# A two-layer decoder trunk on one core: the first layer's output projection of seven token tiles in partial sums in SBUF, beside the last attention pair

## The chip, the cores and the metric

The kernel runs on one core of one Trainium2 chip. The metric is the device time of one execution in microseconds (us). The engines are named as in the profile: PE (TensorE matmuls; PEld its weight loads), DVE (VectorE), ACT (ScalarE), POOL (GpSimd) and SP (SyncE, which here issues every DMA). Each engine works through its own queue in order; semaphores order the queues among each other.

## The reference

1024 tokens of width 1024 pass two layers and a final norm. Layer 0 is causal attention with a forget gate (16 heads of 64), layer 1 a sparse attention ("NSA") with three branches. What matters here is the seam between them:

```
h = rmsnorm(x, norm_g[0]); proj = h @ w_in          # q, k, v, forget gate f, z
o = softmax(q k^T / 8 + c_q - c_k, causal) @ v       # c: running sum of log sigmoid(f)
x = x + (o * silu(z)) @ w_out                        # output projection of layer 0
h = rmsnorm(x, norm_g[1]); proj = h @ nsa_w_in       # layer 1 begins; its first sections are kc and vc
```

## The kernel before, in words

Every float32 product is made of float32r matmuls: an operand is split into a high part (a cast on ACT) and a low part (a subtraction on DVE or POOL), and `mm3` issues three matmuls, hi·hi, hi·lo and lo·hi, into one PSUM bank. Tokens lie in eight tiles t = 0 to 7 of 128; tiles 4 to 7 are half 1, tiles 0 to 3 half 0. A bank holds 128 x 512 float32.

Layer 0's attention goes over eight head pairs p, two heads j each, four query duos x each; a duo joins a long and a short query tile. For each duo PE makes the scores S (six matmuls), DVE adds the gate bias and finds the row minimum (`P`, `m`), ACT takes the exponential and the high part, DVE the low part `hl`, a DMA transposes `hl` into `pT`, and two duos later PE multiplies by v (`O`, 18 matmuls); DVE then scales into `o`. After a pair's last duo PE transposes `o` (`pto`), DVE multiplies with silu(z), and a DMA writes the rows to `oF` in DRAM ("z" in the profile).

Two generators are merged: `fox_main` (the attention) and `fox_fill` (projections k, v, q, z of later pairs, then the weights `wo` of the output projection, then a part of that projection, `out_start`). `merge` takes steps of the filler until their summed cost reaches a ratio (`PACE` = 2.3, and `LAST` = 2.6 for the last eight duos) times the cost of the main steps. A step of the filler may be a condition that blocks it until it holds. Tile's scheduler then sets the final order within each queue.

The output projection needs for a token tile all eight 128-row chunks of `oF`, one per pair: 2 halves of the columns x 8 chunks x 3 = 48 matmuls (named `y`). `out_start` makes for tiles 4 and 5 chunks 0 to 3, then 4 to 6, for tile 6 chunks 0 to 6, and after the last pair chunk 7 of the three. Their sums stay in PSUM all that time, four of its eight banks while scores are still made and six at the end: tile 4 in a bank of `psA` and one of `psS`, tile 5 in `psA` and `psT`, tile 6 in two of `psS`. The attention shares the same pools (S in `psS`, O in `psA`, transposes in `psT`). The other five tiles follow in `out_layer`, behind the attention: load of 8 chunks of `oF` (`of`), split (`ohi`, `olo`), 48 matmuls, addition of x (`xr`, on DVE out of PSUM), sum of squares on ACT, root, reciprocal, two multiplications `h_n` on DVE, then eight transposes (`pth_n`) and their split into `hT` (ACT high, DVE low), which is the input of layer 1. `out_layer` serves layer 1's projection as well. Layer 1 starts with sections `kc` 0, `kc` 1 (PSUM `pn_kc`), each over half 1 and then half 0, 24 matmuls a time; then the gates (`pg`).

Of the kernel before, what the change touches and what calls it, by code (L numbers as in the profile page):

```python
# [19 lines left out]
D = 1024  # L20
S = 1024
# [19 lines left out]
def tile_fox_nsa(ctx, tc, a, out):  # L41
# [216 lines left out]
    hp = tc.alloc_tile_pool(name="hT0", bufs=1, side="right")  # L258
    st = tc.alloc_tile_pool(name="start", bufs=1, side="right")
# [66 lines left out]
    def fox_k(p):  # L326
        KH = [sa.tile([P, S], F32R, tag="KH", bufs=4, name=f"KH_{p}_{j}") for j in range(2)]
        KL = [sa.tile([P, S], F32R, tag="KL", bufs=4, name=f"KL_{p}_{j}") for j in range(2)]
# [111 lines left out]
    def fox_fill():  # L440
        for p in range(8):
# [24 lines left out]
    def out_start():  # L466


        ys = ready["ys"] = {}
        ws = {}  # L470

        def split(t, c, src):
            oh, ol = ws[t]
            A.copy(oh[:, c, :], src)
            V.tensor_tensor(ol[:, c, :], src, f(oh[:, c, :]), OP.subtract)

        def rows_of(t, c):
            yield lambda: ("o", c.stop - 1, 1) in ready
            of = wp.tile([P, KC, P], F32, tag="wst", bufs=1, name=f"of0{t}_{c.start}")
            dma(of[:, c, :], oF[c.start * P:c.stop * P, t * P:(t + 1) * P].rearrange("(k p) t -> p k t", p=P))  # L480
            split(t, c, of[:, c, :])

        def products(t, c):
            oh, ol = ws[t]
            for half in range(2):
                for k in range(c.start, c.stop):
                    wh, wl = ready["wout"][k // 4]
                    cs = slice(half * 512, half * 512 + 512)
                    mm3(ys[t][half], oh[:, k, :], ol[:, k, :], wh[:, k % 4, cs], wl[:, k % 4, cs], k == 0, k == KC - 1)
                    yield 650  # L490

        for t, banks in ((4, (ps_a, ps_s)), (5, (ps_a, ps_t))):
            ws[t] = out_parts(f"0{t}")
            ys[t] = [ps(f"y0_{t}_{half}") for half, ps in enumerate(banks)]
            yield from rows_of(t, slice(0, 4))
# [987 lines left out]
```

## Time and profile before

| | |
|---|---|
| median of 3 runs | 1527.96 us (1526.06 to 1528.8) |
| the profiled execution | 1529.59 us, of which the span of the profile is 1527.8 us |
| busy in the span | PE 1421.9, DVE 1066.2, ACT 805.1, POOL 565.1 us |
| granted TensorE clock over the span | 0.974 |
| 40 to 480 us (attention of layer 0 with its projections) | PE busy 439.17 of 440 us |
| 480 to 590 us (its end) | PE busy 90.12 of 110 us |
| 590 to 672 us (output projection, norms, start of layer 1) | PE busy 74.67 of 82 us |

A group's row gives the busy time, the mean time of one instruction in ns and the idle time of the engine just before it, with what ended that. PE's busy time counts each matmul from its start to its modelled end, and successive matmuls overlap; the distance from start to start is what a matmul costs in a row of them. "PEclk" is the clock that TensorE was granted, as a share of full speed.

### The profile page before, as it was taken

The page shows a single profiled execution, that of the slowest core. Times are in us where ns is not written, and L with a number is a line of the kernel's source. Part 1 is how long each engine was busy: PE and PEld are TensorE (multiplying, and loading weights), DVE is VectorE, ACT ScalarE, POOL GpSimd, SP SyncE. Part 2 cuts the span into 40 slices and gives each one's busy share as a digit, 9 for nine tenths or more (in the row PEclk, how much of TensorE's full clock was granted, in tenths as well). Part 3 has the DMA queues.
Part 4 walks back from the last instruction along what each step waited for, and adds up shares of the span by engine and source line. Part 5 has one row for each costly group of instructions (what it writes and reads, how often), then busy time and mean ns, then how long its engine had stood idle before and what let it go on. Part 6 is the DMA issues. An engine that isn't in the chain of part 4 may idle for free.

```text
span 1527.8 us, 29541 instructions
## 1 busy us (share of the span) xinstructions
PE 1421.9 (93%) x10488; PEld 1179.8 (77%) x10488; DVE 1066.2 (70%) x2759; ACT 805.1 (53%) x2028; POOL 565.1 (37%) x604
## 2 busy tenths in 40 slices
PE   5999999999999778999999899999999999988698
PEld 4888888888788556878888777778888888876576
DVE  6586878788787864457554668677888788888143
ACT  5364646646565652224131664476767676676031
POOL 1232222222322600033333332366767766575000
PEclk9999999999999979999999998999999999999799
DMA  7796777866777765342435577586777857766442
GB/s 254 238 180 142 163 158 157 182 153 143 172 165 166 178 124 197 121 136 83 156 98 163 148 187 201 180 184 133 180 152 146 204 124 144 189 142 147 132 151 83
DMA packets 405812, 242.72 MB, mean 159 GB/s; under 512 B 332513, under 2 KB 353889, under 8 KB 405409
## 3 DMA queue, kind: packets, MB, share of 16 engines
q1 hardware_dynamic: 405664, 240.84, 64.8%
q8 instruction: 83, 1.36, 0.4%
q14 instruction: 65, 0.52, 0.1%
HBM read 120.96 MB, written 44.11 MB: 108 GB/s over the span
## 4 chain that ended last, share of the span: by engine, by line
PE 63%; DVE 16%; ACT 8%; DMA 6%; issue 4%; POOL 1%; SPq 1%; POOLq 0%; DVEq 0%; ACTq 0%
PE S_n L1275 5%; PE y L133 3%; PE y L135 3%; PE y L134 3%; PE ptp_n L1307 3%; ACT P_n L1285 2%; DVE P_n L1282 2%; PE v L133 2%; PE v L135 2%; PE v L134 2%; DVE hl L605 2%; PE S L585 2%; ACT P L603 2%; PE k L133 2%; PE k L134 2%
## 5 line engine op out<-in xcount | busy, mean ns | idle before, releaser
L1285 ACT ACTIVATE P_n<-P_n,m_n 128x640 f32<-128x640 f32 (+7 forms) x256 | 187.2, 732 | 68.5 <-DVE m_n L1282 34.4
L1275 PE MATMUL S_n<-nk,nq 128*128 128x320 f32 (+5 forms) x768 | 180.0, 350 | 8.6 <-DVE m_n L1282 8.3
L603 ACT ACTIVATE P<-P,m 128x512 f32<-128x512 f32 (+1 forms) x192 | 116.9, 610 | 131.4 <-DVE m L594 130.7
L574 POOL TENSOR_TENSOR Bd<-B,tri 128x128 f32<-128x128 f32 x128 | 62.3, 502 | 245.8 <-DVE m L594 227.5
L1289 POOL TENSOR_TENSOR hl_n<-P_n,hl_n 128x640 f16<-128x640 f32 (+4 forms) x128 | 145.0, 1133 | 9.8
L1275 PEld LDWEIGHTS S_n<-nk,nq 128*128 128x128 f32 x768 | 125.2, 193 | 20.9 <-DVE m_n L1282 10.8
L605 DVE SCALAR_TENSOR_TENSOR hl<-P,hl 128x512 f16<-128x512 f32 (+1 forms) x192 | 124.6, 667 | 20.5 <-ACT hl L604 19.5
L1282 DVE CUSTOM_DVE_ANT_0 P_n<-S_n,wmask 128x640 f32<-128x640 f32 (+2 forms) x192 | 113.4, 595 | 25.7 <-PE S_n L1275 16.0
L1288 POOL CAST hl_n<-P_n 128x640 f16<-128x640 f32 (+4 forms) x128 | 77.0, 601 | 122.1 <-ACT P_n L1285 107.8
L150 ACT ACTIVATE pth_n<-ptp_n 128x512 f16<-128x512 f32 (+1 forms) x160 | 85.9, 547 | 49.9 <-PE ptp_n L1307 48.8
L133 PE MATMUL y<-wo,ohi 128*128 128x512 f32 x240 | 97.5, 406 | 15.4 <-ACT ohi L697 13.9
L151 DVE SCALAR_TENSOR_TENSOR ptl_n<-ptp_n,pth_n 128x512 f16<-128x512 f32 (+1 forms) x160 | 99.9, 632 | 15.4 <-ACT pth_n L150 13.9
L1307 PE MATMUL ptp_n<-ident,P_n 128*128 128x128 f32 x576 | 92.4, 281 | 9.4 <-DVE ptl_n L151 4.3
L135 PE MATMUL y<-wo,olo 128*128 128x512 f32 x240 | 95.9, 402 | 0.8 <-DVE olo L698 0.8
L134 PE MATMUL y<-wo,ohi 128*128 128x512 f32 x240 | 96.0, 400 | 0.0
L604 ACT ACTIVATE hl<-P 128x512 f16<-128x512 f32 (+1 forms) x192 | 92.5, 513 | 4.5 <-DMA pT<-hl 3.1
L1307 PEld LDWEIGHTS ptp_n<-ident,P_n 128*128 128x128 f32 x576 | 66.9, 143 | 20.8 <-DVE ptl_n L151 9.5
L585 PE MATMUL S<-KH,Q 128*128 128x512 f32 (+1 forms) x192 | 68.1, 368 | 11.3 <-DVE m L594 10.9
L1315 PE MATMUL O_n<-nv,pth_n 128*128 128x64 f16 x576 | 72.0, 196 | 6.5 <-ACT pth_n L150 5.5
L727 DVE TENSOR_TENSOR xr<-y,xr 128x512 f32<-128x512 f32 x32 | 21.5, 689 | 73.5 <-PE y L135 65.6
L1315 PEld LDWEIGHTS <-pth_n 128*128 128x128 f16 x576 | 52.2, 98 | 25.3 <-ACT pth_n L150 11.1
L1316 PE MATMUL O_n<-nv,pth_n 128*128 128x64 f16 x576 | 71.0, 194 | 0.0
(384 smaller groups left out, 4566.0 us busy)
## 6 DMA issues: line engine op xcount, KB each, us to landing
nq<-qD SPq DMA_DIRECT2D x64, 256.0 KB
B<-cD SPq DMA_DIRECT2D x16, 512.0 KB
wo<-wD SPq DMA_DIRECT2D x16, 512.0 KB
nq<-qD SPq DMA_DIRECT2D x64, 128.0 KB
of<-oF SPq DMA_DIRECT2D x11, 512.0 KB
x<-in_x_dram SPq DMA_DIRECT2D x8, 512.0 KB
wst_k<-in_fox_w_dram SPq DMA_DIRECT2D x8, 512.0 KB
wst_v<-in_fox_w_dram SPq DMA_DIRECT2D x8, 512.0 KB
```

Of the source, the lines that this page charges most:

```text
L133: T.matmul(ps, wh, mh, start=first, stop=False, **kw)
L134: T.matmul(ps, wh, ml, start=False, stop=False, **kw)
L135: T.matmul(ps, wl, mh, start=False, stop=last, **kw)
L151: V.scalar_tensor_tensor(lo[:, 0:n], pt[:, 0:n], scale, h, OP.mult, OP.subtract)
L603: A.activation(L[:, 0:n], L[:, 0:n], AF.Exp, bias=init, scale=-1.0, accum_out=self.lr[:, col + c:col + c + 1])
L605: V.scalar_tensor_tensor(lo[:, cs], L[:, 0:n], UP, hi[:, cs], OP.mult, OP.subtract)
L1275: T.matmul(ps[:, b, 0:w], self.q[x][:, qi * P:(qi + 1) * P], k[:, k0 + b * w:k0 + b * w + w], start=(x == 0), stop=(x == 1))
L1282: V.tensor_tensor_reduce(dst, src, mk, 1.0, 3e38, OP.add, OP.min, m)
L1285: A.activation(L, L, AF.Exp, bias=m, scale=-1.0, accum_out=self.l[:, y, qi:qi + 1])
L1289: G.tensor_tensor(hl[:, n:2 * n], L, hl[:, 0:n], OP.subtract)
L1307: T.transpose(pt[:, (x + i) * P:(x + i + 1) * P], L[:, kb * P - k0:(kb + 1) * P - k0], ident)
L1315: T.matmul(o, hi, v[:, 0:64], start=first, stop=False)
```

## The change

The partial sums no longer wait in PSUM. For each part of the projection (tiles 4 to 7 with chunks 0 to 3, tiles 4 to 7 with chunks 4 to 6, tiles 0, 1, 2 with chunks 0 to 6: eleven parts) the sum goes into a bank of `psA`, and DVE adds it at once to the tile's x row in SBUF (`xs0[t]`, loaded beforehand into the buffers of keys no longer needed, for which `KH` and `KL` move to a pool `sk` of their own that lives longer). Behind the attention stands `out_rest`: for tiles 4, 5, 6, 7 chunk 7 alone, for tile 3 all eight chunks, for tiles 0, 1, 2 chunk 7, with the norm of each tile. The rows of the last pair are loaded once, as two halves (`o7h`, `o7l`), rather than taken from `z` or read back with each tile. The weights `wo` are split with every second subtraction on DVE rather than all on POOL, and the load of their first half moves between two projections. `LAST` goes, and `merge` gets a cap. In layer 1 `kc` 0 and 1 (and `vc` 0 and 1) become one section each: half 1 of both, then half 0 of both.

```diff
-                for half in (1, 0):
-                    yield from fox_q(p, wq, (half,))
-                    yield from fox_z(p, wz, (half,))
-                    yield from load_wout(hp, 0, half)
-        yield from out_start()
+                yield from fox_q(p, wq, (1,))
+                yield from fox_z(p, wz, (1,))
+                rows0 = load_wout(hp, 0, 1)
+                yield next(rows0)
+                yield from fox_q(p, wq, (0,))
+                yield from rows0
+                yield from fox_z(p, wz, (0,))
+                yield from out_start(load_wout(hp, 0, 0))
...
+        parts = [(t, 0, 4) for t in (4, 5, 6, 7)] + [(t, 4, 7) for t in (4, 5, 6, 7)] + [(t, 0, 7) for t in (0, 1, 2)]
...
+        def met(n):
+            t, _, stop = parts[n]
+            return (("o", stop - 1, t // 4) in ready and ("scored", 6) in ready
+                    and (t >= 4 or "scores" in ready))
+        def load(n):
+            t, k, stop = parts[n]
+            if t not in xs0:
+                xs0[t] = sk.tile([P, D], F32, tag=("KH", "KL")[t % 2], name=f"xr0_{t}")
+                dma(xs0[t], a["x"][t * P:(t + 1) * P, :])
+            pend[n] = wp.tile([P, KC, P], F32, tag="wst", bufs=1, name=f"of0_{t}_{k}"), *out_parts(f"0_{t}_{k}")
+            dma(pend[n][0][:, k:stop, :], oF[k * P:stop * P, t * P:(t + 1) * P].rearrange("(k p) t -> p k t", p=P))
...
             for half in range(2):
...
+                if soon:
+                    (load, split)[half](n + 1)
+                pt = ps_a(f"y0_{t}_{k0}_{half}")
+                for k in range(k0, stop):
+                    mm3(pt, oh[:, k, :], ol[:, k, :], wh[:, k % 4, cs], wl[:, k % 4, cs], k == k0, k == stop - 1)
+                    yield 650
+                V.tensor_tensor(xs0[t][:, cs], pt, xs0[t][:, cs], OP.add)
...
-                (V if i else G).tensor_tensor(lo[:, k, cs], f(lo[:, k, cs]), f(hi[:, k, cs]), OP.subtract)
+                (V if i or c else G).tensor_tensor(lo[:, k, cs], f(lo[:, k, cs]), f(hi[:, k, cs]), OP.subtract)
...
-    PACE, LAST = 2.3, 2.6
+    PACE = 2.3
-            if n == len(duos) - 8:
-                yield (LAST,)
-    merge(fox_main(), fox_fill(), PACE, rebase=True)
+    merge(fox_main(), fox_fill(), PACE, rebase=True, cap=4000)
...
+    def out_rest(ow, w, after):
+        dma(gB, a["norm_g"][1:2, :].to_broadcast([P, D]))
+        lh, ll = (ow.tile([P, D], F32R, name=f"o7{x}") for x in "hl")
+        for half in (1, 0):
+            dma(f(ll[:, cols2[half]]), oF[7 * P:8 * P, cols2[half]])
...
+        for t in (4, 5, 6, 7, 3, 0, 1, 2):
...
+            for half, cs in enumerate(cols2):
+                pt = (ps_s, ps_a)[t % 2](f"y0_{t}_{half}")
+                if t == 3:
+                    for k in range(7):
+                        mm3(pt, oh[:, k, :], ol[:, k, :], wh[:, k % 4, cs], wl[:, k % 4, cs], k == 0, False)
+                mm3(pt, lh[:, tk], ll[:, tk], wh[:, 3, cs], wl[:, 3, cs], t != 3, True)
+                V.tensor_tensor(xs0[t][:, cs], pt, xs0[t][:, cs], OP.add)
+                nm.square(cs)
+            pend.append((t, xs0[t], nm.finish(gB, 2)))
+            if len(pend) > 2:
+                after(*pend.pop(0))
...
-        yield from section([(kind, i)], use)
+        yield from section([(kind, 0), (kind, 1)], use)
```

PE's queue of before at the scores of the last pair (`S_7_1_1`: pair 7, head 1, duo 1; `y0_6_4_1` further down: tile 6, chunks from 4, second half of the columns):

```order
L585 MATMUL S_7_1_1_1_0_6588<-KH_7_1_5317,Q_7_0_1_5968 128x384
L586 MATMUL S_7_1_1_1_0_6588<-KL_7_1_5319,Q_7_0_1_5968 128x384
L585 MATMUL S_7_1_1_0_1_6601<-KH_7_1_5317,Q_7_1_1_5745 128x256
L586 MATMUL S_7_1_1_0_1_6601<-KL_7_1_5319,Q_7_1_1_5745 128x256
L619 LDWEIGHTS pT_7_0_3_6461
L619 MATMUL O_7_0_3_6619<-v_7_5526,pT_7_0_3_6461 128x128
```

The same place of the changed kernel:

```order
L134 MATMUL y0_6_4_1_6689<-wo0_0_1_6105,ohi0_6_4_6583 128x512
L135 MATMUL y0_6_4_1_6689<-wo0_0_0_6104,olo0_6_4_6584 128x512
L594 MATMUL S_7_1_1_1_0_6704<-KH_7_1_5320,Q_7_0_1_5955 128x384
L595 MATMUL S_7_1_1_1_0_6704<-KL_7_1_5322,Q_7_0_1_5955 128x384
L594 MATMUL S_7_1_1_0_1_6717<-KH_7_1_5320,Q_7_1_1_5748 128x256
L595 MATMUL S_7_1_1_0_1_6717<-KL_7_1_5322,Q_7_1_1_5748 128x256
L594 MATMUL S_7_1_1_0_0_6723<-KH_7_1_5320,Q_7_1_1_5748 128x512
L595 MATMUL S_7_1_1_0_0_6723<-KL_7_1_5322,Q_7_1_1_5748 128x512
L133 MATMUL y0_6_4_1_6689<-wo0_0_0_6104,ohi0_6_4_6583 128x512
```

Where scores and products with v of the last pair stood alone, matmuls of the projection now stand on both sides of the scores.

DVE's queue of the changed kernel at duo 7_0_3, from its last row minimum on (`xr0_4` is the partial sum of tile 4):

```order
L603 ISA P_7_0_3_0_0_6535,m_7_0_3_0_6527<-S_7_0_3_0_0_6534,B_7_0_6161,m_7_0_3_0_6527 128x512
L603 ISA m_7_0_3_0_6527 128x1
L517 TENSOR_TENSOR xr0_4_6129<-y0_4_4_0_6497,xr0_4_6129 128x512
L517 TENSOR_TENSOR xr0_4_6129<-y0_4_4_1_6552,xr0_4_6129 128x512
L637 TENSOR_TENSOR l_7_0_3_6512<-l_7_0_3_6512 128x1
L638 RECIPROCAL l_7_0_3_6512<-l_7_0_3_6512 128x2
L614 SCALAR_TENSOR_TENSOR hl_7_0_3_6510<-P_7_0_3_0_1_6529,hl_7_0_3_6510 128x512
```

Between a duo's row minimum and the low part that its DMA waits for now stand two additions out of PSUM, the second of which waits for twelve matmuls of `y0_4_4` behind the duo's scores.

PE's queue of before at the seam to layer 1 (`pth_n1_3`: transposes of tile 3's norm; `pn_kc0_1`: section kc 0, half 1):

```order
L135 MATMUL pn_kc0_1_7472<-hT1_1_0_6901,wlo_nkc0_7463 128x512
L116 MATMUL pth_n1_3_0_7398<-ident_72,h_n0_3_7315 128x128 x4
L133 MATMUL pn_kc0_1_7472<-hT1_1_0_6901,whi_nkc0_7462 128x512
L116 MATMUL pth_n1_3_1_7405<-ident_72,h_n0_3_7315 128x128 x4
L134 MATMUL pn_kc0_1_7472<-hT1_1_1_6902,whi_nkc0_7462 128x512
```

And of the changed kernel:

```order
L135 MATMUL y0_2_1_7421<-wo0_0_0_6104,o7l_7148 128x512
L116 MATMUL pth_n1_3_0_7399<-ident_72,h_n0_3_7270 128x128 x4
L116 MATMUL pth_n1_3_1_7406<-ident_72,h_n0_3_7270 128x128 x4
L116 MATMUL pth_n1_0_0_7433<-ident_72,h_n0_0_7346 128x128 x4
L116 MATMUL pth_n1_0_1_7440<-ident_72,h_n0_0_7346 128x128 x4
L133 MATMUL pn_kc0_1_7544<-hT1_1_0_7140,whi_nkc0_7528 128x512
```

The transposes of several tiles, which stood 48 matmuls apart, now follow each other, and four tiles' transposes stand at or behind the end of the projection rather than one.

More of the change, by code (lines that the diff above doesn't have):

```diff
@@ L487, in products @@
                     wh, wl = ready["wout"][k // 4]
-                    cs = slice(half * 512, half * 512 + 512)
-                    mm3(ys[t][half], oh[:, k, :], ol[:, k, :], wh[:, k % 4, cs], wl[:, k % 4, cs], k == 0, k == KC - 1)
+                    mm3(pt, oh[:, k, :], ol[:, k, :], wh[:, k % 4, cs], wl[:, k % 4, cs], k == k0, k == stop - 1)
                     yield 650
[L492 to L495, printed above, removed]
-            yield from products(t, slice(0, 4))
@@ L497, in out_start @@
-        for t in (4, 5):
-            yield from rows_of(t, slice(4, 7))
-        ws[6] = [sa.tile([P, S], F32R, tag=x, bufs=4, name=f"o06_{x}").rearrange("p (k t) -> p k t", k=KC) for x in ("KH", "KL")]
-        yield from rows_of(6, slice(0, 7))
-        for t in (4, 5):
-            yield from products(t, slice(4, 7))
-        yield lambda: "scores" in ready
-        ys[6] = [ps_s(f"y0_6_{half}") for half in range(2)]
-        yield from products(6, slice(0, 7))
-        yield lambda: ("o", 7, 1) in ready
@@ L507, in out_start @@
-        for t in (4, 5, 6):
-            split(t, slice(7, 8), ready["z", 7, 1][1][:, (t - 4) * P:(t - 3) * P].rearrange("p (k t) -> p k t", k=1))
-        for t in (4, 5, 6):
-            yield from products(t, slice(7, 8))
+                V.tensor_tensor(xs0[t][:, cs], pt, xs0[t][:, cs], OP.add)
+            if more and not soon:
+                yield lambda n=n: met(n + 1)
+                load(n + 1)
+                yield 1000
+                split(n + 1)
     def out_parts(name):
@@ L681, in out_layer @@
+    def out_layer(ow, w, src, res, g, after, name, early):
         gB = ow.tile([P, D], F32, name=f"gB{name}")
         dma(gB, g.to_broadcast([P, D]))
-        pend, first = [], list(ready.get("ys", {}))
-        bufs = 4 if first else 2
-        cs = [slice(half * 512, half * 512 + 512) for half in range(2)]
+        pend = []
         def tiles(t):
-            if not early:
-                return out_tiles(f"{name}_{t}")
             of = ow.tile([P, KC, P], F32, tag="of", bufs=3, name=f"of{name}_{t}")
@@ L730, in out_layer @@
             pend.append((t, xt, h))
-            for _ in range(0 if t in first else 2):
-                if len(pend) > 1:
-                    after(*pend.pop(0))
+            if len(pend) > 1:
+                after(*pend.pop(0))
         for x in pend:
@@ L1159, in nsa_fill @@
     def nsa_fill():
-        for i in range(2):
-            yield from cmp_raw("kc", i)
+        yield from cmp_raw("kc")
         yield from gate_sec()
```

100 lines of the change are left out of this document (58 added, 42 removed).

## The prediction

> **What bounds it now.** I read the totals first, then stretches, then PE's waits in the stretch that changes. Two rows of the totals and two of the forty slices:
>
> ```profile
> PE 1421.9 (93%) x10488; PEld 1179.8 (77%) x10488; DVE 1066.2 (70%) x2759; ACT 805.1 (53%) x2028; POOL 565.1 (37%) x604
> ...
> PE 5999999999999778999999899999999999988698
> ...
> PEclk9999999999999979999999998999999999999799
> ```
>
> PE is the bound nearly everywhere; slices 14 to 16 (497 to 611 us) are a hole, with a dip of the clock. The next view gives busy time by stretch: from 40 to 480 us; from the scores of the last duo of pair 6 (502.92) to the first product of chunk 7 (585.78); from there to the gate section of layer 1 (686.88):
>
> ```profile
> core 0: us, PE busy (x) PEld busy (x) DVE busy (x) ACT busy (x) POOL busy (x), PEclk, DMA share, GB/s
> 40.00:480.00 440.00, 439.17 (x2700) 361.24 (x2699) 342.08 (x1014) 242.72 (x601) 123.61 (x136) 1.00 0.75 166
> 502.92:585.78 82.86, 62.98 (x395) 48.54 (x394) 53.09 (x172) 42.15 (x109) 23.25 (x28) 0.86 0.60 128
> 585.78:686.88 101.10, 93.77 (x422) 76.26 (x421) 49.84 (x88) 31.57 (x71) 13.54 (x12) 0.95 0.49 166
> ```
>
> In the first row PE never stops although DVE is busy 342/440 = 78%. In the second PE idles 19.9 us and runs at 0.86 of its clock; in the third it idles 7.3 us at 0.95. What PE waited for in the last two stretches together (who, for whom: us in total, times, longest):
>
> ```profile
> PE S L585 <- DVE m L594: 10.9, 9, 4.5
> PE y L133 <- ACT ohi L697: 4.7, 2, 2.4
> PE O L619 <- DMA pT<-hl: 3.8, 2, 2.0
> PE O L619 <- DVE ot L631: 2.8, 2, 2.4
> ```
>
> These are latencies of the chain of one duo, which nothing covers once the filler has run out, not an engine that is full: DVE is busy 53.1 of 82.9 us.
>
> **What PE has to do.** Durations from start to start, at full clock: 48 matmuls of the projection (the stretch of tile y alone); then, each by its first row and the row behind it, four transposes `pto`, one duo's scores, its product with v, and a tile's eight transposes `pth`:
>
> ```profile
> 627.24:638.25 11.01, 11.01 (x48) 8.91 (x48) 0.80 (x2) 1.00 0.30 95
> ```
>
> ```profile
> 463.96 0.60 PE L641 MATMUL pto<-ident,o 128*128 128x128 f32 x4
> 464.31 0.48 PE L133 MATMUL v<-hT,whi_v 128*128 128x512 f32 x1
> ...
> 470.32 0.28 PE L585 MATMUL S<-KH,Q 128*128 128x256 f32 x1
> 471.37 0.40 PE L133 MATMUL v<-hT,whi_v 128*128 128x512 f32 x1
> ...
> 474.11 0.23 PE L619 MATMUL O<-v,pT 128*128 128x128 f16 x1
> 474.89 0.47 PE L133 MATMUL q<-hT,whi_q 128*128 128x512 f32 x1
> ...
> 638.25 1.03 PE L116 MATMUL pth_n<-ident,h_n 128*128 128x128 f32 x8
> 639.04 0.47 PE L133 MATMUL y<-wo,ohi 128*128 128x512 f32 x1
> ```
>
> So 0.229 us a matmul, 1.05 a duo's scores, 0.78 its product, 0.35 and 0.79. By PE's queue of before, 502.92 to 585.78 holds 9 duos' scores (9.5), 11 products (8.6), 16 pto (1.4) and 126 y (28.9): 48.4 us of work in 82.9. The stretch behind it holds 258 y (59.1), 64 pth (6.3) and 96 matmuls of kc (22.0): 87.4 in 101.1. Together 135.8 us of work in 184.0: 48 us are lost, 27.2 of them idle, the rest to the clock. The changed queue has the same work between the same two points, so 48 us is the most that the change can bring there; what it brings is 48 less what it leaves lost.
>
> **Stage one: the partial sums beside the last pair.** PE: 9.5 + 8.6 + 1.4 + 294 y x 0.229 = 67.3, together 86.8 us. On DVE the change adds 22 additions out of PSUM, of which none stood in this stretch. The rows of additions, norms and splits, the first six over 592 to 690 us, the others over 480 to 592 us (the groups by shape: busy us, mean ns, idle before):
>
> ```profile
> L106 DVE SCALAR_TENSOR_TENSOR h_n<-xr,st_n,gB 128x512 f32<-128x512 f32 x16 | 11.5, 766 | 0.1
> L121 DVE TENSOR_TENSOR hT<-pth_n,hT 128x512 fp32r<-128x512 f32 x16 | 10.7, 684 | 0.4 <-ACT hT L120 0.4
> L727 DVE TENSOR_TENSOR xr<-y,xr 128x512 f32<-128x512 f32 x16 | 10.7, 688 | 19.9 <-PE y L135 16.2 <-DMA xr<-in_x_dram 3.7
> ...
> L100 DVE TENSOR_TENSOR st_n<-st_n 128x1 f32<-128x1 f32 x8 | 2.4, 309 | 0.2 <-ACT h_n L94 0.2
> L128 DVE CAST whi_nkc<-wst_nkc 128x1024 fp32r<-128x1024 f32 x2 | 1.4, 695 | 9.0 <-PE y L134 9.0
> ...
> L102 DVE RECIPROCAL st_n<-st_n 128x1 f32<-128x1 f32 x8 | 1.2, 156 | 1.0 <-ACT st_n L101 1.0
> ...
> L475 DVE TENSOR_TENSOR olo<-of,ohi 128x512 fp32r<-128x512 f32 x2 | 1.3, 672 | 0.0
> L475 DVE TENSOR_TENSOR olo<-of,ohi 128x384 fp32r<-128x384 f32 x2 | 1.1, 556 | 0.2 <-ACT ohi L474 0.2
> L475 DVE TENSOR_TENSOR o_KL<-of,o_KH 128x896 fp32r<-128x896 f32 x1 | 1.1, 1093 | 1.5 <-ACT o_KH L474 1.5
> ```
>
> 22 x 0.688 = 15.1. Splits: 3 x 0.67 + 4 x 0.56 + 4 x 1.09 + 2 x 0.67 for the last rows = 9.9, against 0.67 + 2 x 0.56 + 1.09 = 2.9 now: +7.0. Four subtractions of `wo` of the eight that DVE gets fall here. DVE has 53.1 + 15.1 + 7.0 + 3.6 = 79 us to do while PE has 86.8. That is the crowded part: evenly spread it fits, but the adds stand in DVE's queue ahead of the low parts `hl` on which DMA, transposed `pT` and O wait, and an add waits for its PE matmuls (up to 21 x 0.229 = 4.8 us). The price of that is not in the trace. Bounds: 0.2 us of stall, as in 40 to 480 us (0.83 idle in 440), and 20 us, today's idle time of this stretch. I take 10, the middle: the DVE share would be 79/97 = 81%, close to the row without stalls, but DVE's first half is denser (12 of the 22 adds and all four `wo` subtractions).
>
> [...] The POOL and DVE rows from a split of `wo` now:
>
> ```profile
> 498.38 2.71 POOL L537 TENSOR_TENSOR wo<-wo,wo 128x512 fp32r<-128x512 f32 x2
> 498.67 1.28 DVE L605 SCALAR_TENSOR_TENSOR hl<-P,hl 128x256 f16<-128x256 f32 x1 [0.99 <-ACT hl L604]
> ...
> L537 DVE TENSOR_TENSOR wo<-wo,wo 128x512 fp32r<-128x512 f32 x16 | 14.2, 890 | 2.8 <-ACT wo L536 2.8
> ```
>
> Two POOL subtractions take 2.71 us and a DVE low part that starts under them 1.28. The third row is layer 1's split, which DVE does under a busy POOL (1330 to 1410 us): 0.89 us each. I sum 4 x 0.89 = 3.6. [...]
>
> DMA: seven loads of x rows and more loads of `of` now stand among the transposes on SP; those of x for tiles 4 and 5 come just ahead of pair 7's bias row and of `wo`, for which ACT waits with the exponentials behind it. A delay of 1 to 2 us from that is within the 10. POOL loses eight subtractions, which helps DVE alone. `LAST` and the cap only set the order that the queues show; that no sum sits in `psS` any more gives the scores, which wait 10.9 us, all three banks. ACT gets the casts of the same parts: it is busy 42.2 of 82.9 us and I cost it at nothing, covered by its idle half.
>
> **Between the stages.** The rows of the last pair must reach DRAM and come back. The chain now (start, length, what):
>
> ```profile
> 584.64 0.76 DVE z L643
> ...
> 585.42 2.03 DMA oF<-z
> ...
> 587.47 3.97 DMA of<-oF
> ```
>
> 0.76 + 2.03 + 3.97 and a split in two steps, each taken as the 0.67 of the L475 row: 8.1 us. Behind the last `pto` PE has 63 y = 14.4 us: hidden, where today 4.7 us go in two waits for `ohi`.
>
> **Stage two: chunk 7, tile 3, norms.** PE: 48 + 42 y (20.6), 64 pth (6.3), then 48 matmuls of kc for half 1 (11.0), which need only tiles 4 to 7: 37.9 us until kc wants half 0. DVE: 16 adds 11.0, 16 h 11.5, 16 hT 10.7, the small ones of the norm 2.4 + 1.2, two casts 1.4: 38 us. The two are level, and they alternate. By hand, in queue order: PE's first transposes come after 34 matmuls (7.8 us) while DVE needs 8 adds, small ones and two h, some 8.5: 1 us lost. Behind the last product of tile 3, DVE owes five adds, six hT, four h and small ones (11.4 us) until tile 3's second hT, and PE's transposes of tile 0 wait for that (two banks of `psT`), with kc stuck behind them in the queue; PE has 6.9: 4.5 lost. Tiles 1 and 2 lose 0.7 and 1.4. With the seams I take 8 (bounds: 1, the wait before the first transposes alone; 16, twice my count, if each ACT step between two DVE steps shows).
>
> **The clock.** It falls without long pauses:
>
> ```profile
> 528.00:532.00 4.00, 3.69 (x48) 1.00 0.27 49
> 532.00:536.00 4.00, 1.57 (x8) 1.00 1.06 146
> 536.00:540.00 4.00, 2.19 (x8) 0.51 1.04 220
> 540.00:544.00 4.00, 4.00 (x25) 0.64 0.11 32
> ```
>
> After 4 us with 1.57 busy the clock is half and stays so into the next 4 us, fully busy. In the changed kernel stage one should hold the full clock; the 4.5 us loss of stage two may cost one such drop. I take 3 us (0 to 8). [...]
>
> **Elsewhere.** The order behind kc is the same but for vc (both halves swapped likewise) and a few places at the end of layer 1, where `wo` of layer 1 is paced without eight pauses: 0, bounds -2 and +2.
>
> **Sum.** 48 lost now; left 10 + 8 + 3 = 21; gain 27 against the profiled execution (1529.6, which stands 1.6 above the median): median 1527.96 - 27, rounded to 1501.
>
> **Rivals.** (a) Everything hides: stage one as free as 40 to 480 us (3), stage two 5, clock 0: gain 40, 1488. For it: DVE at 81%; against: adds that wait in the middle of DVE's queue. (b) DVE sets stage one's pace and stage two's: 17 + 12 + 5 = 34 left, gain 14, 1514. For it: 79 us of DVE under 87 of PE, in order. (c) Slower: each add holds DVE's queue until its matmuls are done, so a duo's `hl`, `pT` and O come late, O stands ahead of the next filler on PE, and both alternate instead of overlapping. It decides where the 22 adds cost PE more than (48 - 11)/22 = 1.7 us each; at 2 us, 44 + 11 = 55 are left and it ends 7 us up, at 1535. Against: while an add waits, PE works on the very matmuls that it waits for, and two duos lie between a duo's scores and its product. (d) It does not do what it says: the parts wait for `oF` and `of` (one buffer) and run behind the pair after all. For it: load 4.0 and split 1.1 us a part against 18 x 0.229 = 4.1 of PE; against: scores and products fill the rest of a part's time. Stage one then keeps 19.9 idle and 0.14 x 82.9 = 11.6 of clock, with 11 behind it: gain 5, 1523.
>
> **Chances.** Forecast (1494 to 1508) 0.55, (a) 0.13, (b) 0.23, (d) 0.05, (c) 0.04. 1489 to 1515 holds the forecast, most of (a) and most of (b): 0.8. Three us, 0.2%, is about what a measurement of this kernel tells from no change; a hundredth each of (c) and (d) ends within it: faster 0.95, within 0.02, slower 0.03.
>
> **What would show it.** Right: PE busy nearly all of 503 to 600 us at clock 1.0; y between S and O; kc's start of half 0 near 649 us (502.9 + 86.8 + 10 + 37.9 + 8 + 3); waits of `pth` on DVE of 5 to 8 us. Wrong: `PE O <- DMA pT` or `PE y <- DVE olo` of over 10 us in stage one, or DVE over 90% busy there with PE under 85%.

## The result, and the profile after

The changed kernel takes 1518.79 us (median of four runs) against 1527.2 for the kernel before on the same chip: ratio 0.9934, 95% interval 0.9917 to 0.9951. Run again it came to 0.9927 (0.9910 to 0.9944). The gain is 8 to 11 us where 27 were forecast; 1518.8 lies outside the range of 1489 to 1515.

Two rows of the totals after, and two of the forty slices (each now 37.9 us):

```profile
PE 1417.8 (93%) x10488; PEld 1177.1 (78%) x10488; DVE 1079.6 (71%) x2790; ACT 804.2 (53%) x2029; POOL 552.9 (36%) x596
...
PE   5999999999999898999999999899999999898698
...
PEclk9999999999999999999999999999999999998799
```

Slices 14 to 16, which read 7, 7 and 8 before, read 8, 9 and 8: the hole is about half closed. Where a lead over the kernel before is won and lost is read best from two points that both traces have: the first matmul of the gate section and the first of layer 1's output projection. Before:

```profile
686.88 0.39 PE L1010 MATMUL pg<-hT,gw 128*128 128x512 f32 x1
```

```profile
1429.17 0.80 PE L133 MATMUL y<-wo,ohi 128*128 128x512 f32 x1 [9.26 <-ACT ohi L697]
```

After:

```profile
667.67 0.39 PE L1047 MATMUL pg<-hT,gw 128*128 128x512 f32 x1
```

```profile
1419.03 0.80 PE L133 MATMUL y<-wo,ohi 128*128 128x512 f32 x1 [9.36 <-ACT ohi L739]
```

At the gate section the changed kernel is 19.2 us ahead (predicted 27), at the end of layer 1's attention 10.1. So the miss against the forecast has two parts of about equal size: 8 us not won at the seam, and 9 us given back in layer 1, where the prediction had put 0.

The seam after, by stretch (the columns are those of the prediction's stretches):

```profile
480.00:516.00 36.00, 29.39 (x191) 23.15 (x190) 27.80 (x86) 23.45 (x58) 10.68 (x14) 0.91 0.92 220
516.00:600.00 84.00, 77.70 (x481) 62.56 (x480) 60.35 (x175) 37.32 (x93) 10.57 (x16) 0.96 0.77 172
600.00:634.00 34.00, 34.00 (x164) 28.02 (x162) 22.69 (x43) 14.49 (x36) 5.84 (x4) 1.00 0.40 132
634.00:667.67 33.67, 30.30 (x142) 24.60 (x142) 22.39 (x42) 13.69 (x32) 8.05 (x9) 0.95 0.50 161
```

The prediction's 48 us lost less 19.2 leaves 29. PE's idle time makes 16.3 of them: 6.6 in the first row, 6.3 in the second, 3.4 in the last. At half clock PE ran in the equivalent of (1 - 0.91) x 36 + (1 - 0.96) x 84 + (1 - 0.95) x 33.67, about 8 us more; some 4 us stand in no row. The kernel before had no hole ahead of 503 us:

```profile
480.00:502.92 22.92, 22.92 (x161) 18.57 (x159) 17.32 (x54) 15.65 (x38) 9.49 (x11) 1.00 1.00 215
```

After, one begins at 495. Its making, on DVE, ACT and PE (start, length, what, in brackets the idle time before it and what ended that):

```profile
493.96 0.08 DVE L603 DVE_READ_ACCUMULATOR2_ANT m<- 128x1 f32 x1
498.43 1.34 DVE L547 TENSOR_TENSOR wo<-wo,wo 128x512 fp32r<-128x512 f32 x1 [4.39 <-ACT wo L546]
499.70 0.74 DVE L603 CUSTOM_DVE_ANT_0 P<-S,B,m 128x512 f32<-128x512 f32 x1
```

```profile
497.26 1.14 ACT L546 CAST wo<-wo 128x512 fp32r<-128x512 f32 x2 [5.80 <-DMA wo<-wD]
```

```profile
500.50 0.50 PE L594 MATMUL S<-KH,Q 128*128 128x512 f32 x1 [2.26 <-DVE m L603]
```

DVE stands 4.39 us before a subtraction of `wo`, which waits for ACT, which waits 5.80 us for the weights; a row minimum stands behind it on DVE, and PE's scores wait for that. PE's two largest waits from 480 us to the gate section (who, for whom: us in total, times, longest):

```profile
PE S L594 <- DVE m L603: 7.4, 5, 2.3
PE O L628 <- DMA pT<-hl: 3.5, 2, 2.4
```

What PE waited for in layer 1, of its waits from the gate section on, those that the kernel before doesn't have (who, for whom: us in total, times, longest):

```profile
PE S_n L1310 <- DMA nk<-kD: 1.8, 1, 1.8
...
PE hid_vc L133 <- ACT bh_vc L880: 1.5, 1, 1.5
PE hid_kc L133 <- ACT bh_kc L880: 1.4, 1, 1.4
```

### The profile page after: what moved, and what is told of

It is laid out like the page before. It is cut to its first block, busy times and chain, and to the rows that moved or that the text cites. A ratio compares the mean times of both kernels' runs of the same rounds, so it can differ in the third digit from the quotient of the medians.

```text
span 1517.1 us, 29572 instructions
## 1 busy us (share of the span) xinstructions
PE 1417.8 (93%) x10488; PEld 1177.1 (78%) x10488; DVE 1079.6 (71%) x2790; ACT 804.2 (53%) x2029; POOL 552.9 (36%) x596
## 4 chain that ended last, share of the span: by engine, by line
PE 61%; DVE 15%; ACT 9%; DMA 7%; issue 4%; POOL 2%; SPq 1%; POOLq 0%; DVEq 0%; ACTq 0%
PE S_n L1310 5%; PE y L133 3%; PE y L134 3%; PE y L135 3%; PE ptp_n L1342 3%; ACT P_n L1320 2%; PE v L133 2%; PE v L135 2%; PE v L134 2%; DVE P_n L1317 2%; PE k L133 2%; PE S L594 2%; PE k L134 2%; PE k L135 2%; DMA of<-oF 2%
## 5 line engine op out<-in xcount | busy, mean ns | idle before, releaser
L614 DVE SCALAR_TENSOR_TENSOR hl<-P,hl 128x512 f16<-128x512 f32 (+1 forms) x192 | 121.4, 651 | 16.8 <-ACT hl L613 15.9
L1317 DVE CUSTOM_DVE_ANT_0 P_n<-S_n,bias 128x640 f32<-128x640 f32 (+1 forms) x64 | 65.1, 1017 | 7.5 <-PE S_n L1310 7.3
```

Of the source, the lines that this page charges most:

```text
L614: V.scalar_tensor_tensor(lo[:, cs], L[:, 0:n], UP, hi[:, cs], OP.mult, OP.subtract)
L1317: V.tensor_tensor_reduce(dst, src, mk, 1.0, 3e38, OP.add, OP.min, m)
```

## The experiments: layer 1

Times below are medians; a ratio is to the kernel before, run beside it on the same chip, with its 95% interval. "Lost" is the time of a stretch less its nominal matmul time, each recorded matmul priced from start to start as in the prediction (0.229 us, and 1.05, 0.78, 0.35 and 0.79 for the groups); a few records are missing, so it is good to 1 us. How far single executions differ is larger than that: seven of the profiles below (the changed kernel twice, and five of kernels that change only what stands behind 600 us) have the same queue of PE up to there, and from 480 to 600 they lose 21.9 to 24.7 us, with 12.9 to 15.0 us of idle time. Six of them, all but the one of the kernel with a lag of one tile, reach the gate section at 665.4 to 668.5. A difference inside these spreads tells nothing.

**The changed kernel again.** No edit.

> The changed kernel once more, nothing edited. In its first profile it reached the gate section 19.2 us ahead of the kernel before (667.67 against 686.88) and ended 10.1 us ahead (first y of layer 1 at 1419.03 against 1429.17): 9 us are given back in layer 1, in steps of 1.2 (hid_kc), 1.4 (hid_vc), 3.1 (start of the attention, 969 to 988), 1.2 (near 1192) and 2.5 (1330 to 1410). Theory A (order: the merged kc and vc and the projection weights without pauses cost it every time): the same five steps, time 1517 to 1521. Theory B (chance: where a short pause falls in the windows of the clock gate, and DMA landing): the steps at 969, 1192 and 1330 move or vanish by 2 us or more, while the two at hid_kc and hid_vc stay; runs spread over 1513 to 1521.

1518.65 us, ratio 0.9927 (0.9910 to 0.9944), runs from 1513.5 to 1521.85. The gate section came at 666.95, 19.9 us ahead, the first y at 1418.91, 10.3 ahead. All five steps were there again, to within 0.6 us when the last is read at the first y: A, as far as one more execution tells.

**Single sections.** The merge of kc and vc undone, all else as changed:

```diff
-        yield from section([(kind, 0), (kind, 1)], use)
+        yield from section([(kind, i)], use)
...
-        yield from cmp_raw("kc")
+        for i in range(2):
+            yield from cmp_raw("kc", i)
```

> The changed kernel with kc 0, kc 1 and vc 0, vc 1 as single sections again, half 1 and half 0 of each, as before the change. Theory A (the merged sections hide the late norms of tiles 0 to 2 behind 48 matmuls rather than 24, and cost 1.4 us at hid_kc and 1.5 at hid_vc, since the compressed branch gets its last rows at once): the two waits on bh_kc and bh_vc fall from 1.4 and 1.5 to 0.3 or less, and the gate section starts 2 to 5 us later than 667.7; end to end -1 to +3 us against the changed kernel. Rival (the merge hides nothing, because the transposes of tiles 0 to 2 stand ahead of kc in the queue anyway): the gate section starts within 1 us of 667.7 and the kernel ends 2 to 3 us earlier, near 1516.

1511.0 us, ratio 0.9887 (0.9870 to 0.9904); the interval does not touch that of the changed kernel beside it. Run once more, as the reference of the third group, it came to 1513.43 and 0.9906 (0.9886 to 0.9926), which does overlap with it. The two waits on `bh` are gone, and the gate section comes no later:

```profile
665.99 0.39 PE L1050 MATMUL pg<-hT,gw 128*128 128x512 f32 x1
```

The rival has the mechanism right: the merge hid nothing, since the transposes of tiles 0 to 2 stand ahead of kc in the queue in any case. From the first chunk-7 product to the gate section both kernels take 55.4 us. Its size was too small: it said 2 to 3 us, and on the same chip the merge cost 7.7 us (1518.65 against 1511.0); by the ratios of the two runs of each kernel it is 3 to 7. The two waits explain 2.6 of them in the lead (1.2 and 1.4); the other part shows in no single wait.

**The pauses back.**

```diff
                 (V if i or c else G).tensor_tensor(lo[:, k, cs], f(lo[:, k, cs]), f(hi[:, k, cs]), OP.subtract)
+            if i:
+                yield 200
```

> The changed kernel with the pauses (200 per chunk) back in the loading of layer 1's projection weights. Theory A (without them the casts and subtractions for the weights crowd the last attention groups and cost the 2.5 us lost between 1330 and 1410): that step of the lead goes and the time falls by 2 to 3 us, to 1516. Theory B (the clock gate's windows fall differently by chance there): within 1.5 us of the changed kernel, and the half clock near 1386 comes or goes whatever the pauses.

1515.07 us, ratio 0.9914 (0.9899 to 0.9928), overlapping the changed kernel's. The step between 1330 and 1410 stayed (2.3 us), and two windows at half clock were still there near 1381. That is against A, although the median came out 3.6 us below the changed kernel's beside it, as A would have it; within these intervals the time does not decide.

**The two edits of layer 1 alone, on the kernel before.**

> The kernel before with the two edits of layer 1 alone: kc and vc merged, and the projection weights of layer 1 loaded without the pauses. The prediction's own step says 0, from -2 to +2, downstream. Theory A (these two edits give back what layer 0 gains): the waits on bh_kc and bh_vc appear here too (1.4 and 1.5 us), the steps near 1190 and 1330 to 1410 as well; the gate section starts 0 to 5 us earlier (half 0 of kc comes 24 matmuls later, behind the norms); in all +1 to +6 us from the gate section to the end. Theory B (they cost only the two waits, the rest is chance of the clock gate): +2.6 us from the gate section to the end, give or take 1.7 us for one window at half clock.

1533.42 us, ratio 1.0033 (1.0022 to 1.0045): slower, by 5 us. This is the prediction's "elsewhere" by itself, merge and missing pauses together. The two waits are there:

```profile
PE hid_vc L133 <- ACT bh_vc L841: 1.4, 1, 1.4
PE hid_kc L133 <- ACT bh_kc L841: 1.4, 1, 1.4
```

Behind each of them the clock falls for one window (692.87 and 785.02), and the two places cost 2.7 and 2.9 us there.

**Both undone, the seam as changed.**

> The changed kernel with both edits of layer 1 undone: kc and vc single sections, and the pauses back in the loading of layer 1's projection weights; layer 0 and the seam stay as changed. Theory A (the two edits cost what they cost alone, 7.6 and 3.6 us): 1507 to 1508, the lead of 20 to 21 us at the gate section is kept to within 2 us at the first y of layer 1. Rival (the pauses and the merge share one cost, the last stretch of the attention): 1510 to 1512, no better than the single sections alone (1511.0).

1514.25 us, ratio 0.9902 (0.9882 to 0.9923): no better than single sections alone. No cost of the missing pauses shows here; the merge is the edit that costs. From the gate section to the first y this kernel and the three beside it, which have the same layer 1, took 746.4, 744.2, 741.6 and 747.8 us, the single sections 745.4 and 745.9, the kernel before 742.3, the changed kernel 751.4 and 752.0, and the kernel with the pauses back, which keeps the merge, 748.2. So of the 9 us given back some 2 to 6 are the merge.

Another part is not layer 1's edits at all. Between 950 and 1205 us (on the time of the kernel before) the changed kernel loses 4.2 us of its lead, but the single sections lose 3.4 there (2.4 when run again) and the kernel with both edits undone 3.5, while the kernel before with the two edits loses 0.1. The wait on `nk` shown above goes with it: 16 of the 18 profiles with the changed seam have it (0.8 to 2.0 us), the two without the changed seam do not. In the single sections:

```profile
PE S_n L1315 <- DMA nk<-kD: 1.5, 1, 1.5
```

So this part, 2 to 4 us, comes into layer 1 along with the changed seam; why the load comes late there stays open. What happens behind 1300 us differs from execution to execution.

## The experiments: the seam

**wo split on POOL again** (with layer 1 as before the change, as the next two).

```diff
-                (V if i or c else G).tensor_tensor(lo[:, k, cs], f(lo[:, k, cs]), f(hi[:, k, cs]), OP.subtract)
+                (V if i else G).tensor_tensor(lo[:, k, cs], f(lo[:, k, cs]), f(hi[:, k, cs]), OP.subtract)
```

> As the kernel with layer 1 as before the change, and all subtractions of layer 0's wo on POOL again. In the changed kernel DVE stood 4.39 us in front of its first wo subtraction (498.43), which waits for ACT's cast, which waits for the DMA of wo; the row minimum of the next duo stood behind it in DVE's queue, and PE's scores waited 2.26 us for that. Theory A (this head-of-line wait makes the hole at 495 to 513): the waits of S on m at 500, 508 and 510 (5.5 us in all) fall below 2 us, the gate section starts 3 to 6 us earlier than in the kernel with layer 1 as before. Rival 1 (the hole is the end of the filler: only z of pair 7 is left beside the last duos of pair 6, whoever subtracts): the same start within 1.5 us. Rival 2 (POOL then blocks DVE's low parts and wo comes late): 1 to 4 us later, with waits of y on wo.

1516.72 us, ratio 0.9923 (0.9903 to 0.9944), gate section at 671.16 against 668.51 for its reference. PE's waits of this kernel from 480 us to its gate section:

```profile
PE y L133 <- ACT ohi L495: 5.3, 2, 4.4
PE O L630 <- DVE ot L642: 2.8, 1, 2.8
PE S L596 <- DVE m L605: 2.6, 3, 1.4
```

The waits on m did fall, from 7.6 to 2.6 us, as A says, but what they lost came back as waits on `ohi` and `ot`. Rival 2 has the end right (2.7 us later), though y waited for the rows `ohi` and not for the weights. In the profile before, low parts that started under one of POOL's subtractions of `wo` took longer: of 128x512, 0.94 to 1.07 us (three) against 0.68 with no POOL instruction beside them (median of 87); of 128x256, 1.09 and 1.28 against 0.42 (median of 24).

**The first split behind z.**

```diff
-                yield from rows0
                 yield from fox_z(p, wz, (0,))
+                yield from rows0
```

> As the kernel with layer 1 as before the change, but the split of the first half of wo (casts on ACT, subtractions on DVE and POOL) stands behind the z projection of half 0 of pair 7 rather than ahead of it; its DMAs stay where they are. Theory A (the casts wait 5.8 us for the DMA of wo at 491 to 497 with the exponentials behind them on ACT, and the subtraction does the same to the row minima on DVE): both waits go, S waits less than 2 us in 495 to 513, the gate section 3 to 6 us earlier, unless the first y (513.98) now waits for the weights. Rival (the weights come too late): y starts 3 us or more later, and the gate section 1 to 4 us later.

1514.16 us, ratio 0.9904 (0.9884 to 0.9924), gate section at 669.58. The wait at 500 fell to 0.99 us, and the next, at 508, grew from 1.31 to 2.65. The same picture: the wait moves one duo on. The first y starts no later (512.95 against 513.49), so the weights did not come too late either, and still the gate section is 1.1 us later.

**A lag of one tile in stage two.** `len(pend) > 1` for `> 2` in `out_rest`.

> As the kernel with layer 1 as before the change, but each tile's transposes follow one tile behind its sum rather than two. The prediction counted 8 us of stall in stage two, 4.5 of them where the transposes of tile 0 wait for DVE; measured are 3.4 us of waits from 634 to 642 and one window at half clock. Theory A (with the longer lag PE's queue holds enough products; the shorter one makes it wait for each norm): waits of pth on h_n of 3 to 6 us more, gate section 3 to 6 us later. Rival (DVE's total work sets the end of stage two, whatever the lag): within 1 us.

1514.65 us, ratio 0.9911 (0.9892 to 0.9930), gate section at 667.17, 1.3 us earlier than its reference, with waits of `pth` on `h_n` of 3.9 us in place of 2.0. The 1.3 us are won ahead of stage two, where the two queues are the same. From the first chunk-7 product to the gate section it takes 56.0 us, inside the 54.5 to 56.2 of the eleven profiles with the longer lag and all the work in them (the last two kernels below left aside). So A is out, and the rival's "within 1 us" holds for stage two; that DVE's work is what sets its end fits this and is not shown by it.

**The filler spread otherwise.** The single sections again as reference, then the steps that give PE nothing priced at 0, then a lower ratio for the last twenty duos, then both:

> The changed kernel with single kc and vc sections once more, as the reference for the three runs beside it: 1510 to 1515, gate section at 665 to 668. PE's nominal work from 480 to 516 us is 25.8 of 36: 10 us are lost there, with S waiting 2.3, 1.3 and 2.0 us for m and 6.8 us at half clock.

```diff
-                yield 400 if i else 200
+                yield 400 if i else 0
...
         load(0)
-        yield 2000
+        yield 0
```

> As the single sections, with the steps of layer 0's filler that give PE nothing priced at 0 in the merge: the splits of wo (8 steps of 200 each half) and the wait behind the first load (2000). In the queue of the changed kernel these 1600 and 2000 take the place of matmuls: between the products of duo 6_0_3 and the scores of 6_1_2 stand 3 matmuls where its neighbours have 9 to 12, between the scores of 6_1_3 and the products of 6_1_1 none. Theory A (the hole at 495 to 513 is these missing matmuls: PE gets its scores too early and waits for m): the first wait on m (2.3 us) goes, the lost time of 480 to 516 falls from 10 to 6 or 7, the gate section starts 2 to 5 us earlier, time 1508 to 1511. Rival (DVE and the DMA of wo set the pace of the chain there): the wait moves to the next duo, the gate section within 1.5 us of its start without this edit.

```diff
+            if n == len(duos) - 20:
+                yield (2.0,)
             if n < len(duos):
```

> As the single sections, with the merge's ratio at 2.0 rather than 2.3 for the last twenty duos, so that the projections of pair 7 last until the partial sums may start: matmuls of z then stand on both sides of the scores of 6_1_2, 6_1_3 and 7_0_0. Theory A (the hole is the filler's end): the lost time of 480 to 516 falls from 10 to 3 to 5, the gate section 4 to 7 us earlier, time 1505 to 1508. Rival 1 (with less filler per duo the chain of a duo shows earlier, from 370 us on): idle time of 3 us or more before 480 us, and the end unchanged. Rival 2 (the chain of DMA, DVE and ACT at 490 to 515 is late in itself): S waits for m as long as before.

> Both edits, the prices at 0 and the ratio 2.0 for the last twenty duos, with single sections: at every place between 470 and 520 us 6 to 12 matmuls then stand between scores and products. Theory A (the filler's end and its empty prices make the hole): the lost time of 480 to 516 falls from 10 to 3 us or less, the gate section at 659 to 661, where the prediction put the gain of the seam (27 us), time 1503 to 1507. Rival (DVE's chain): no more than 2 us earlier than 666.

| | median us | ratio | lost 480 to 516 | lost 516 to 600 | gate section |
|---|---|---|---|---|---|
| single sections | 1513.43 | 0.9906 (0.9886 to 0.9926) | 10.0 | 11.8 | 665.92 |
| prices 0 | 1514.5 | 0.9909 (0.9886 to 0.9932) | 10.5 | 14.1 | 669.73 |
| ratio 2.0 | 1517.62 | 0.9934 (0.9913 to 0.9956) | 6.7 | 20.1 | 670.08 |
| both | 1516.83 | 0.9929 (0.9906 to 0.9953) | 5.3 | 19.2 | 667.41 |

The two rows of the kernel with the ratio, 480 to 516 and 516 to 600:

```profile
480.00:516.00 36.00, 31.62 (x210) 24.70 (x209) 30.07 (x89) 23.77 (x60) 11.15 (x14) 1.00 0.97 228
516.00:600.00 84.00, 72.42 (x431) 57.85 (x430) 59.04 (x162) 35.46 (x86) 11.51 (x14) 0.88 0.67 157
```

With the prices at 0 the first wait on m fell from 2.35 to 1.00 us and the next grew from 1.31 to 2.64. With the ratio, matmuls between scores and products do fill the first hole (PE busy 31.62 of 36, clock 1.00), and the idle time comes back behind it: PE then idles 11.6 of 84 us at 0.88. My reading that the hole is the end of the filler fails for the stage as a whole: the loss of 480 to 600 is 22 to 27 us however the filler is spread, and the gate section comes no earlier than in the six profiles above.

**What of the added work makes it.** Three kernels that each leave one part of the added work out, and one that leaves out all three; the matmuls stay. One run each, so the profile is what counts, and it is held against the spread of the seven profiles above.

```diff
-                V.tensor_tensor(xs0[t][:, cs], pt, xs0[t][:, cs], OP.add)
```

> The changed kernel with single kc and vc sections, with DVE's 22 additions of the partial sums into the x rows left out (the eleven parts are computed and dropped; chunk 7 and tile 3 are added as before). PE's lost time from 480 to 600 us is 21.8 to 22.0 with the additions, whichever way the filler was spread (22 to 27 over five kernels). Theory A (the additions hold DVE's queue, and with it the row minima, low parts and products of the last pair): 10 us or more of the loss goes. Theory B (the splits of wo and of the loaded rows on ACT and DVE are what is late): 3 us or less goes. Theory C (the duo's own chain, ACT, DVE, DMA transposes, is the pace when the filler's matmuls stand in the wrong places): 3 us or less.

```diff
+                if not i:
+                    continue
                 A.copy(hi[:, k, cs], f(lo[:, k, cs]))
...
-        ready.setdefault("wout", []).append((hi, lo))
+        ready.setdefault("wout", []).append((hi, lo) if i else (lo, lo))
```

> As the single sections, with layer 0's split of wo left out: no casts on ACT, no subtractions on DVE or POOL, both operands read the weights as they were loaded; every matmul and DMA stays. Theory B (the split at 497 to 520 holds ACT and DVE behind the DMA of wo): the loss of 480 to 516 falls from 10 to 5 or less, and that of 480 to 600 by 5 us or more. Theories A and C: 2 us or less of 480 to 600.

```diff
+            if n:
+                pend[n] = pend[0]
+                return
             pend[n] = wp.tile([P, KC, P], F32, tag="wst", bufs=1, name=f"of0_{t}_{k}"), *out_parts(f"0_{t}_{k}")
```

> As the single sections, with the loading and splitting of rows left out for the ten parts behind the first: all parts use the rows of the first; the matmuls, additions and x loads stay. Theory B for these splits (DVE's 9.9 us of them, ACT's casts and ten DMAs on SP among the transposes): 5 us or more of the 22 us lost from 480 to 600 goes, most of it at 530 and behind 565. Theories A and C: 3 us or less.

> As the single sections, with all three left out: additions, split of wo, loading and splitting of rows. What then stays lost from 480 to 600 us is the duos' own chain and the order of PE's queue. Theory C (the chain and the order): 12 us or more of the 22 stay, with waits of S on m and of O on the transposes at the ends of the two pairs. Theories A and B (the added work on DVE and ACT): 5 us or less stay, and the gate section starts near 650.

| left out | lost 480 to 516 | lost 516 to 600 | together | gate section | time us |
|---|---|---|---|---|---|
| nothing (reference) | 10.0 | 11.8 | 21.8 | 665.92 | 1513.43 |
| additions | 10.7 | 15.4 | 26.1 | 670.46 | 1516.16 |
| split of wo | 4.3 | 14.3 | 18.6 | 662.32 | 1506.02 |
| rows' loads and splits | 10.2 | 8.6 | 18.8 | 663.33 | 1504.55 |
| all three | 6.9 | 7.6 | 14.5 | 660.35 | 1504.81 |

The stretch 516 to 600 of the reference, of the kernel without the additions, and of the one without all three:

```profile
516.00:600.00 84.00, 75.64 (x484) 60.59 (x483) 60.30 (x173) 36.69 (x91) 10.42 (x16) 1.00 0.80 177
```

```profile
516.00:600.00 84.00, 75.36 (x466) 60.12 (x465) 51.25 (x156) 37.68 (x93) 11.51 (x16) 0.96 0.81 169
```

```profile
516.00:600.00 84.00, 80.68 (x501) 66.46 (x500) 41.21 (x141) 28.63 (x75) 5.33 (x12) 0.96 0.70 160
```

PE's waits from 480 to 600 us, two of the reference and the largest of the kernel without all three:

```profile
PE S L594 <- DVE m L603: 7.5, 6, 2.4
PE O L628 <- DMA pT<-hl: 5.0, 4, 3.1
```

```profile
PE O L634 <- DMA pT<-hl: 7.2, 3, 3.3
```

DVE's busy time falls from 60.30 to 51.25 us without the additions, and PE is no better off (why the loss came out 4 us larger in this one run is not explained): theory A, the one on which the prediction's term and its slower rival rested, falls. Each of the two splits costs about 3 us, just outside the spread of 21.9 to 24.7, and less than the 5 us that theory B asked for (though without the split of `wo` 480 to 516 did fall to 4.3, as B said). With DVE at 41.21 of 84, 14.5 us still stay lost, within theory C's 12 or more. But only one of the two waits that C named stays: those of O on `pT` (2.7 and 3.3 us at the ends of the two pairs, 1.2 ahead of them). The waits of S on m are gone, so these come from the added work, as far as one run tells. Idle time falls from 15.0 to 7.5 us; the loss falls by less, since PE stands at half clock for three windows there and for one in the reference. And of the 7.3 us won up to 600 the gate section keeps 5.6.

**Matmuls ahead of the last products.** A condition in the main generator, `yield lambda: ("part", 9, 0) in ready` ahead of the last step, and in the second kernel the ratio 1.8 for the last eight duos:

> As the single sections, with the first half of the part of tile 1 (21 matmuls, and the 4 that were left of tile 0) put ahead of the products of the last duo rather than behind them: 45 matmuls stand there where 17 stood, and none is added. In the kernel without it PE waits 3.1 to 3.5 us there for the transposes of that duo, with 63 matmuls of the projection behind the wait in its queue. Theory C (order: the matmuls stand on the wrong side of a wait): the wait goes, the loss of 516 to 600 falls from 11.8 to 8 or 9, the gate section at 662 to 664. Rival (the loss moves on: what was put ahead is missing as cover for the last pair's rows): a wait of the chunk-7 products of 2 to 4 us, the gate section within 1 us of 666.

> As the run beside it, and the merge's ratio 1.8 rather than 2.3 for the last eight duos, so that the parts of tiles 4 to 7 last until the parts of tiles 0 to 2 may start: 9 matmuls then stand on both sides of the scores of 7_1_2 and 7_1_3, where 0 to 3 stood. Theory C (order): the waits of S on m at 567 to 576 (2 to 3 us, and what they cost in clock) go too; loss of 516 to 600 down to 6 or less, the gate section at 659 to 661, time 1506 to 1509. Rival (the duos' chain is the pace, and comes late wherever the matmuls stand): the gate section at 664 or later.

1516.1 us, 0.9919 (0.9899 to 0.9939), and 1517.03, 0.9928 (0.9908 to 0.9948); gate section at 669.65 and 669.68. The first kernel's two waits:

```profile
583.08 0.23 PE L629 MATMUL O<-v,pT 128*128 128x128 f16 x1 [2.88 <-DMA pT<-hl]
```

```profile
612.44 0.59 PE L133 MATMUL y<-wo,o7h 128*128 128x512 f32 x1 [2.89 <-ACT o7h L703]
```

The edit missed its aim: in the queue the products that wait are those of the last duo but one, and the matmuls were put behind these. The old wait stayed, and what was moved was missing as cover for the last pair's rows, the rival's mechanism: up to 600 us it loses 21.0 us, no more than the reference, and the gate section comes 3.7 us later, beyond the rival's 1 us. The first kernel therefore does not tell order from chain. In the second the waits of S on m at 567 to 576 did go, and no time with them; the same wait on `pT` (3.20 us) came at 578. Whether the right order could save it was not tried.

## Why the prediction was wrong, by its steps

- **48 us lost, latency not engines.** Right as to what could be won: the seam gave 19.2 of them, and DVE went from 53.1 to 68.0 us of the 82.9 from 502.92 on without being what PE waits for all the time.
- **Stage one, 10 us (0.2 to 20), and its reason: the failed step at the seam.** Idle there is 12.9 us, near the 10, but its clock costs 6 to 7 more, and the whole loss, by the nominal count, is 23 (10.5 + 12.5). That the idle time came near the 10 is luck, since the reason was wrong: leaving out the additions saves nothing. The splits of `wo` and of the rows cost some 3 us each; 14.5 us of the loss and 7.5 us of the idle time stay with all three gone, as waits of O on its transposes and as clock. Whether that rest is the chain of the duo itself or the order of PE's queue stays open. I started the stage at 502.92, where the scores stood, and so did not look at 495 to 503, where the moved load of `wo` now stands. The 3.6 us for four subtractions on DVE were their length; the eight on record from 480 to 600 took 0.83 us each, near my 0.89, but the first waited 4.39 us with a row minimum behind it. I had asked that question for the additions, and not for the subtractions.
- **The x loads and `wo` on SP, 1 to 2 us.** Somewhat small: ACT waited 5.80 us for the first chunk of `wo`, and PE's scores behind it 2.26.
- **Between the stages, hidden.** Right: from 600 to 634 us PE is busy 34.00 of 34.
- **Stage two, 8 us.** Idle is 3.4 us, with one window at half clock: 6 in all. The count by queue order was right in kind (2.0 on `h_n`, 1.4 on `hT`), and twice too high in size: the 8 was stall alone, the clock being a term of its own.
- **Clock, 3 us (0 to 8).** About 8 us: five windows at half clock from 480 to 668, four of them in stage one, which I had taken to hold the full clock.
- **Elsewhere, 0 (-2 to +2): the other failed step.** Alone, on the kernel before, it measures +5 us. I took a merged section for a mere change of order. It hands the compressed branch all its rows at once, so that `hid_kc` and `hid_vc` wait for ACT; and I counted 48 matmuls of kc as cover in stage two, where single sections take the same 55.4 us. The 2 to 4 us lost between 950 and 1205 are in no term: I took layer 1 behind the same queue to run as before.
- **Rivals.** The time lies between (b) at 1514 and (d) at 1523, by neither mechanism. (c), slower by the additions, is excluded by leaving them out.
- **The signs.** Half 0 of kc starts at 656.8 us, not 649; `pth` waits 3.4 us on DVE, not 5 to 8; and neither sign of being wrong came (O waits 3.5 us for `pT`, DVE is 82% busy from 502.92 to 585.78). The wait that did come, S on m with 7.4 us, was on neither list, though it was the largest before as well.

Of the kernels with all the work in them the one with single sections has the lowest ratio, 0.9887, and 0.9906 when run again, against 0.9934 and 0.9927 for the changed kernel; its second run is no better than both undone (0.9902) or the split behind z (0.9904).

## What to carry to other kernels

When work moves next to a chain of short steps, cost what stands in front of each queue, not only what is added to it: leaving out the split of `wo`, whose first subtraction waits 4 us at the head of DVE's queue, took some 3 us off the loss, and leaving out 22 additions none. Where several ways of filling a hole only move the wait, measure by leaving work out, several times over; four runs told here that the added work makes about half of the idle time, and which part of it does not count. And test the small edits that come along with a large one by themselves: here one of them took back about a third of the gain.

## What the runs showed of the hardware

The granted clock changes on a raster of 3.41 us (in the profile of the changed kernel its changes from 509.08 to 1512.60 us lie whole multiples of 3.413 us apart), and the clock of a window went, but for the cases near the border that the table below counts, with how busy PE was in the window before it. Four windows in a row of the changed kernel, and then two pairs of windows:

```profile
505.67:509.08 3.41, 1.62 (x8) 0.97 (x6) 3.31 (x9) 3.21 (x7) 2.75 (x3) 1.00 0.60 116
509.08:512.49 3.41, 1.92 (x4) 1.01 (x4) 3.41 (x15) 1.69 (x5) 1.01 (x3) 0.50 0.43 110
512.49:515.91 3.42, 3.42 (x24) 3.03 (x24) 3.36 (x13) 3.42 (x11) 0.70 (x1) 0.50 0.94 324
515.91:519.32 3.41, 3.41 (x18) 2.83 (x17) 1.60 (x5) 3.01 (x7) 1.29 (x1) 1.00 1.01 226
```

```profile
570.52:573.93 3.41, 1.64 (x20) 1.08 (x17) 3.41 (x16) 1.29 (x3) 0.00 (x0) 1.00 0.86 209
573.93:577.34 3.41, 3.34 (x22) 2.71 (x23) 3.15 (x12) 3.38 (x11) 0.00 (x0) 0.50 0.52 114
...
580.76:584.17 3.41, 1.38 (x8) 0.89 (x6) 2.11 (x5) 1.23 (x4) 0.00 (x0) 1.00 1.17 265
584.17:587.58 3.41, 3.04 (x22) 2.76 (x23) 0.72 (x2) 0.00 (x0) 0.00 (x0) 0.50 1.10 207
```

A window with PE busy 1.62 or 1.64 of 3.41 us (48%) is followed by one at half clock, though the longest pause inside it is 1.3 or 1.4 us. Counted over all twenty profiles of this study, windows from 60 to 1400 us:

| this window | PE busy in it | next at half | next at full |
|---|---|---|---|
| full clock | under 0.45 | 135 | 1 |
| full clock | 0.45 to 0.50 | 36 | 14 |
| full clock | 0.50 to 0.70 | 24 | 190 |
| full clock | 0.70 and over | 0 | 7166 |
| half clock | under 0.85 | 68 | 0 |
| half clock | 0.85 and over | 15 | 188 |

The length of the longest pause tells less: the best single limit on it (1.5 us) puts 83 of the full-clock windows on the wrong side, the best limit on the busy share (0.51) 38. So by this table two pauses of 1 us that fall into one window (41% busy; 135 of 136 such windows had one at half clock behind them) cost a window at half clock, up to 1.7 us more (half of 3.41, an estimate); the same two on both sides of a border (71% busy each; none of 7166) cost nothing more. That may be a source of the 4 to 9 us by which runs of one kernel differ here, since the raster does not start with the kernel: counted from the start of the span, its borders lie at 0.1 to 3.4 us in the twenty profiles. This was only argued.
